# Long scans and an earlier gate row in the mLSTM gate chain, and the operand loads of the second MLP product on another queue

## The chip, the core and the metric

The kernel runs on one core of a Trainium2 chip. The core has a matrix engine (TensorE, PE in the profile), three engines for elementwise work (VectorE or DVE, ScalarE or ACT, GpSimd or POOL), and a fifth, SyncE or SP, which here only issues DMA transfers; ScalarE can issue them too. Each engine works through its instructions in order, and semaphores hold it where it needs another's result. The metric is the device time of one execution in microseconds, the median of several runs.

## The reference, cut to what matters

```python
def _layer(x, c_act, ...):                      # x: 1024 positions x 1024, one sequence
    sh1, sc1, g1, sh2, sc2, g2 = split(c_act @ w_ada + b_ada, 6)
    h = ln(x) * (1 + sc1) + sh1
    q, k, v, o, fz, gates = split(h @ w_in)
    mix = concat([mlstm(q, k, v, o, gates), fourier(fz)]) @ w_out
    x = ln_affine(ALPHA * x + (1 + g1) * mix, ln1_g, ln1_b)
    h2 = ln(x) * (1 + sc2) + sh2
    ff = square(relu(h2 @ w_ff1 + b_ff1)) @ w_ff2 + b_ff2      # 1024 -> 4096 -> 1024
    return ln_affine(ALPHA * x + (1 + g2) * ff, ln2_g, ln2_b)

# in mlstm, for each of 4 heads and two directions, chunk after chunk of 128 positions:
    b = cumsum(log_f)                  # within the chunk
    g = b[-1] - b + log_i
    m_new = max(b[-1] + m, g.max())    # running stabiliser
    C = exp(b[-1] + m - m_new) * C + sum_s exp(g - m_new)[s] * k[s] v[s]^T
```

The cumulative sums of the forget gate, the running maximum of log_i - b, the per-chunk stabiliser m and the exponentials that come from them are the gate chain. All values are float32.

## The kernel before

Every float32 product is done as three matmuls on numbers split in a high and a low half: hi by hi (line 133), hi by lo (line 134), lo by hi (line 135). A split is a cast to the high half on ScalarE (line 1204 in the second MLP product) and a subtraction for the low half on VectorE (line 1205).

The stages follow one another: layer norm and modulation, its transpose, the products with w_in, the gate chain, the chunk states C and the mLSTM output per head, the Fourier groups, w_out, layer norm, the first MLP product, the second MLP product, layer norm. The order of the instructions on each engine is made by a scheduler with a timeline of its own, within the dependencies of the code; so code that is written in another place need not stand in another place on an engine, and an edit in one place can shift instructions elsewhere.

**Gate chain (lines 449 to 536).** Forget gates Fz and input gates I are transposed to 64 rows (32 forward, 32 backward) by 1024 positions, and copied out of PSUM (line 456). Lines 461 to 464 make log_sigmoid. The sums are taken chunk by chunk, 128 positions at a time: 16 scans of 32x128 (lines 468 and 470), a subtraction (line 472), and 16 more for the maximum (lines 476 and 478). Then come steps of 8 elements per row (lines 489 to 499), the maximum of cm with m0 (line 507), and the row I (line 506), which TensorE transposes (line 522). With what comes of that, VectorE makes kw (line 559) and the states C (lines 574 and 578); line 634 is the first product with the states. While the chain runs, TensorE does products with w_in that were kept for that time.

**Second MLP product (lines 1195 to 1348).** The product is computed by seven smaller products p, in the order 1, 2, 5, 6, 3, 7, 4. Each has eight units u, a unit has a left operand (hraw, read back from hid_d in DRAM, line 1221) and a right one (raw, from w_ff2, line 1212), both split, and 24 matmuls. The left loads are all issued by ScalarE, the right ones by SP. After p = 1 the code loads the layer norm's rows lg2 and lb2, makes the gate row g2 (line 680, from b_ada and g), gb = b_ff2 * g2 (line 1344), and loads the eight tiles acc with x2, each followed by acc = ALPHA * acc + gb (line 1347). gb lies in one of the three buffers of the raw loads.

Of the kernel before, what the change touches and what calls it, by code (L numbers as in the profile page):

```python
# [9 lines left out]
F32 = mybir.dt.float32  # L10
F32R = mybir.dt.float32r
AF = mybir.ActivationFunctionType
ALU = mybir.AluOpType

P = 128
D = 1024
# [74 lines left out]
def body(ctx, tc, x, c, w_ada, b_ada, w_in, b_gate, norm_w, w_out, ln1_g, ln1_b,  # L91
# [359 lines left out]
    for k_, dst in ((1, Fz), (0, I)):  # L451
        for hf in range(2):
            pt = bank("c")
            for i in range(4):
                nc.tensor.transpose(out=pt[0:64, i * P:(i + 1) * P], in_=zg[:, hf * 4 + i, k_, :], identity=ident)
            nc.vector.tensor_copy(out=dst[0:64, hf * 512:hf * 512 + 512], in_=pt[0:64, :])
# [9 lines left out]
    for n in range(NC):  # L466
        f, r_ = slice(n * P, n * P + P), slice(n * P + P - 1, n * P - 1 if n else None, -1)
        nc.vector.tensor_tensor_scan(out=br[0:32, f], data0=on[0:32], data1=Fr[0:32, f], initial=0.0,
                                     op0=ALU.mult, op1=ALU.add)
        nc.vector.tensor_tensor_scan(out=br[32:64, r_], data0=on[32:64], data1=Fr[32:64, r_], initial=0.0,  # L470
                                     op0=ALU.mult, op1=ALU.add)
    nc.vector.tensor_sub(out=a_, in0=a_, in1=br)
    cm = Fr
    for n in range(NC):
        f, r_ = slice(n * P, n * P + P), slice(n * P + P - 1, n * P - 1 if n else None, -1)
        nc.vector.tensor_tensor_scan(out=cm[0:32, f], data0=a_[0:32, f], data1=a_[0:32, f], initial=-3e38,
                                     op0=ALU.max, op1=ALU.max)
        nc.vector.tensor_tensor_scan(out=cm[32:64, r_], data0=a_[32:64, r_], data1=a_[32:64, r_], initial=-3e38,
                                     op0=ALU.max, op1=ALU.max)
# [26 lines left out]
    nc.vector.tensor_tensor(out=I[64:128].rearrange("p (n t) -> p n t", t=P), in0=a_v, in1=bcn(mx), op=ALU.subtract)  # L506
    nc.vector.tensor_tensor(out=cmv, in0=cmv, in1=bcn(m0), op=ALU.max)
# [709 lines left out]
    def left(p, u):  # L1217
        nraw[0] += 1
        pl, t_, n_ = ((r2, "hraw", 2), (opp, "op4", 2))[nraw[0] // 2 % 2] if nraw[0] > 2 else (xp, "raw", 3)
        raw = pl.tile([P, 2, 512], F32, name="hraw", tag=t_, bufs=n_)  # L1220
        nc.scalar.dma_start(out=raw, in_=hid_d[p - 1, 2 * u:2 * u + 2].rearrange("n p d -> p n d"))
        return raw
# [90 lines left out]
    for n_, p in enumerate((1, 2, 5, 6, 3, 7, 4)):  # L1313
        pbs = [bank(t_) for t_ in ("aabc", "abbc")[n_ % 2]]
        late = NLAST if p == 4 else 0
        for u in range(NU - late):
# [3 lines left out]
            if p == 3:  # L1320
                raw = w2_raw(u, 1, 0)
                nc.vector.tensor_sub(out=tt[u], in0=raw, in1=tt[u])
            if p == 7 and u % 2:
                for ch in range(2):
                    ln2_part(u // 2, ch)
                ln2(u // 2)
# [10 lines left out]
        if n_ == 0:  # L1337
            lg2, lb2 = [r2.tile([P, D], F32, name=n) for n in ("lg2", "lb2")]
            nc.sync.dma_start(out=lg2, in_=bc1(ln2_g))
            nc.sync.dma_start(out=lb2, in_=bc1(ln2_b))  # L1340
            gate_rows(1, g2)
            gb = xp.tile([P, D], F32, name="gb", tag="raw", bufs=3)
            nc.sync.dma_start(out=gb, in_=bc1(b_ff2))
            nc.vector.tensor_mul(out=gb, in0=gb, in1=g2)
            for st in range(NST):
                nc.sync.dma_start(out=acc[st], in_=x2_d[st * P:st * P + P, :])
                nc.vector.scalar_tensor_tensor(out=acc[st], in0=acc[st], scalar=ALPHA, in1=gb, op0=ALU.mult,  # L1347
                                               op1=ALU.add)
# [25 lines left out]
```

## Time and profile before

| | |
|---|---|
| median of 3 runs | 1109.8 us (1107.94 to 1109.94) |
| the profiled execution, its own time | 1109.07 us |
| its span, first to last instruction | 1107.3 us |
| TensorE busy | 1042.8 us (94%) |
| VectorE busy | 775.9 us (70%) |
| ScalarE busy | 469.4 us (42%) |
| GpSimd busy | 319.6 us (29%) |
| mean granted TensorE clock | 0.965 of 2.4 GHz |

TensorE is the engine that is nearly always busy, so the time goes where it idles or where its clock is at the lower of its two levels (0.50 of full speed, 1.2 GHz). The shares of the other engines are means over stages that differ; whether VectorE matters is seen only in the stretch where TensorE waits for it. All start times below are microseconds from the start of the span.

### The profile page before, as it was taken

Reading aid. Unit: us, or ns where it says so; the run is one execution under the profiler, and the core shown is the slowest. Engines: PE = TensorE matmul, PEld = TensorE weight load, DVE = VectorE, ACT = ScalarE, POOL = GpSimd, SP = SyncE. Lnnn points to the kernel's source line nnn. Section 1 sums busy time; section 2 is a strip of 40 time slices with the busy share of each in tenths; the row PEclk is TensorE's granted clock in tenths of the full one; section 3 lists DMA queues with packets and bytes.
Section 4 is the critical chain, followed back from the end, with each engine's and each line's share of the span. In section 5 each row is a group of like instructions: output and inputs, shape, how many; then the busy total and the mean of one; then the engine's idle time right before and its main releaser. Section 6 shows DMA issues by size and latency. Waiting matters only on the chain.

```text
span 1107.3 us, 14282 instructions
## 1 busy us (share of the span) xinstructions
PE 1042.8 (94%) x5033; PEld 857.1 (77%) x5033; DVE 775.9 (70%) x1431; ACT 469.4 (42%) x812; POOL 319.6 (29%) x247
## 2 busy tenths in 40 slices
PE   5899989999899898879999999999989999999995
PEld 3788978898677687668888888888868888888884
DVE  7943785967779488878565445445476896668997
ACT  3353125654355115676455445354344333333420
POOL 3554205532124011002777766752200000000000
PEclk7999989989899899989999999999999999999998
DMA  9926604432224802854566564546978885688402
GB/s 307 290 60 216 195 28 122 132 115 89 82 65 137 284 39 102 251 180 125 162 212 206 180 206 150 178 152 204 340 282 288 266 308 190 218 271 282 163 30 93
DMA packets 146887, 199.31 MB, mean 180 GB/s; under 512 B 9392, under 2 KB 74876, under 8 KB 146816
## 3 DMA queue, kind: packets, MB, share of 16 engines
q1 hardware_dynamic: 126688, 162.22, 44.7%
q10 hardware_dynamic: 20128, 36.18, 9.7%
q8 instruction: 39, 0.64, 0.2%
q14 instruction: 32, 0.26, 0.1%
HBM read 153.01 MB, written 45.36 MB: 179 GB/s over the span
## 4 chain that ended last, share of the span: by engine, by line
PE 57%; DVE 2%; ACT 1%; DMA 0%; issue 0%; DVEq 0%; ACTq 0%
PE psb L134 7%; PE psb L135 7%; PE psb L133 7%; PE psa L133 7%; PE psa L134 7%; PE psa L135 7%; PE psc L134 5%; PE psc L135 5%; PE psc L133 5%; DVE acc L1347 0%; PE psc L933 0%; DMA rw<-in_w_ff_dram 0%; DVE acc L1304 0%; ACT b L937 0%; ACT w L955 0%
## 5 line engine op out<-in xcount | busy, mean ns | idle before, releaser
L1204 ACT CAST o<-hraw 128x1024 fp32r<-128x1024 f32 x56 | 58.6, 1050 | 137.1 <-PE psc L135 107.5
L1205 DVE TENSOR_TENSOR o<-hraw,o 128x1024 fp32r<-128x1024 f32 x56 | 70.5, 1265 | 42.2 <-ACT o L1204 42.2
L133 PE MATMUL psa<-wh,hR 128*128 128x256 f32 (+2 forms) x268 | 81.0, 303 | 0.6 <-DVE acc L892 0.6
L135 PE MATMUL psa<-wh,hR 128*128 128x256 f32 (+2 forms) x268 | 79.9, 298 | 0.0
L134 PE MATMUL psa<-wl,hR 128*128 128x256 f32 (+2 forms) x268 | 79.4, 297 | 0.0
L134 PE MATMUL psa<-o,o 128*128 128x512 f32 x176 | 69.3, 394 | 5.9 <-DVE o L1205 5.9
L135 PE MATMUL psa<-o,o 128*128 128x512 f32 x176 | 69.4, 394 | 0.0
L133 PE MATMUL psa<-o,o 128*128 128x512 f32 x176 | 68.9, 393 | 0.0
L978 ACT ACTIVATE hq<-hq 128x512 f32<-128x512 f32 x59 | 37.1, 629 | 62.2 <-DVE hq L974 61.4
L134 PE MATMUL psb<-o,o 128*128 128x512 f32 x160 | 62.9, 393 | 0.0
L135 PE MATMUL psb<-o,o 128*128 128x512 f32 x160 | 62.8, 393 | 0.0
L133 PE MATMUL psb<-o,o 128*128 128x512 f32 x160 | 62.4, 392 | 0.0
L263 POOL TENSOR_TENSOR wl<-raw,wh 128x256 fp32r<-128x256 f32 (+2 forms) x27 | 38.0, 1430 | 73.8 <-ACT wh L262 73.8
L133 PEld LDWEIGHTS psa<-wh,hR 128*128 128x128 f32 x268 | 52.6, 196 | 2.7 <-DVE acc L892 1.3
L134 PEld LDWEIGHTS psa<-wl,hR 128*128 128x128 f32 x268 | 52.6, 196 | 2.0 <-issue 0.9
L135 PEld LDWEIGHTS psa<-wh,hR 128*128 128x128 f32 x268 | 52.4, 196 | 1.0
L1047 DVE TENSOR_TENSOR ws<-raw,ws 128x1024 fp32r<-128x1024 f32 x30 | 39.6, 1333 | 13.8 <-ACT ws L1046 13.8
L418 POOL TENSOR_TENSOR m<-m,mraw 128x512 f32<-128x512 f32 x28 | 39.5, 1412 | 29.6 <-ACT m L415 10.3
L1037 POOL TENSOR_TENSOR raw<-raw 128x512 f32<-128x512 f32 x15 | 21.3, 1418 | 90.4 <-DVE w L1112 86.2
L1204 ACT CAST o<-raw 128x1024 fp32r<-128x1024 f32 x32 | 33.3, 1048 | 31.4 <-DVE raw L1247 18.2
L1171 POOL TENSOR_TENSOR hq<-hq 128x512 f32<-128x512 f32 x16 | 22.7, 1418 | 78.1 <-ACT hq L979 62.1
L134 PEld LDWEIGHTS psa<-o,o 128*128 128x128 f32 x176 | 33.3, 189 | 13.7 <-DVE o L1205 6.3
(437 smaller groups left out, 3150.6 us busy)
## 6 DMA issues: line engine op xcount, KB each, us to landing
raw<-in_w_ff_dram SPq DMA_DIRECT2D x104, 512.0 KB, 4.8
hraw<-hid_d ACTq DMA_DIRECT2D x56, 512.0 KB, 4.8
hid_d<-hq SPq DMA_DIRECT2D x107, 256.0 KB, 3.2
mraw<-in_w_ada_dram SPq DMA_DIRECT2D x32, 512.0 KB, 4.2
raw<-in_w_in_dram SPq DMA_DIRECT2D x10, 512.0 KB, 3.9
xt<-in_x_dram SPq DMA_DIRECT2D x8, 512.0 KB, 5.3
wa<-in_w_ada_dram SPq DMA_DIRECT2D x16, 256.0 KB, 5.2
wa<-in_w_ada_dram SPq DMA_DIRECT2D x8, 512.0 KB, 8.1
```

The source lines that it names most:

```text
L133: nc.tensor.matmul(out=out_ap, lhsT=lh, rhs=rh, start=first, stop=False)
L134: nc.tensor.matmul(out=out_ap, lhsT=lh, rhs=rl, start=False, stop=False)
L135: return nc.tensor.matmul(out=out_ap, lhsT=ll, rhs=rh, start=False, stop=last)
L263: nc.gpsimd.tensor_sub(out=wl, in0=raw, in1=wh)
L418: nc.gpsimd.tensor_add(out=mc, in0=mc, in1=rv[:, i])
L978: nc.scalar.activation(out=h_, in_=h_, func=AF.Relu)
L1037: eng.tensor_add(out=r1[:, hi], in0=r1[:, lo], in1=r1[:, hi])
L1047: nc.vector.tensor_sub(out=w_[:, 1], in0=s_, in1=w_[:, 0])
L1171: nc.gpsimd.tensor_add(out=sa, in0=h12, in1=h22)
L1204: nc.scalar.copy(out=o_[:, 0], in_=raw)
L1205: eng.tensor_sub(out=o_[:, 1], in0=raw, in1=o_[:, 0])
```

## The change

In the gate chain the two copies of I out of PSUM go to ScalarE; the 32 scans over a chunk each become four over all 1024 positions, in which a mask tile, keep, restarts the sum or the maximum at the start of each chunk; and the row I comes ahead of the maximum over cm. In the second MLP product all left loads but the first three are issued by SP; gb has a place of its own, which lb2 takes over later; the eight loads of acc and their additions are written into the loops of p = 2 and p = 5; lg2 and lb2 are loaded after p = 6.

```diff
@@ gate chain
-            nc.vector.tensor_copy(out=dst[0:64, hf * 512:hf * 512 + 512], in_=pt[0:64, :])
+            (nc.vector.tensor_copy if k_ else nc.scalar.copy)(out=dst[0:64, hf * 512:hf * 512 + 512], in_=pt[0:64, :])
...
-    for n in range(NC):
-        f, r_ = slice(n * P, n * P + P), slice(n * P + P - 1, n * P - 1 if n else None, -1)
-        nc.vector.tensor_tensor_scan(out=br[0:32, f], data0=on[0:32], data1=Fr[0:32, f], initial=0.0,
-                                     op0=ALU.mult, op1=ALU.add)
-        nc.vector.tensor_tensor_scan(out=br[32:64, r_], data0=on[32:64], data1=Fr[32:64, r_], initial=0.0,
-                                     op0=ALU.mult, op1=ALU.add)
+    keep = md.tile([64, 2, S], F32, name="keep")
+    for w_, (rest, start) in enumerate(((1.0, 0.0), (0.0, -3e38))):
+        nc.gpsimd.memset(keep[:, w_], rest)
+        nc.gpsimd.memset(keep[:, w_].rearrange("p (n t) -> p n t", t=P)[:, :, 0:1], start)
+
+    def scans(out, src, which, initial, op0, op1):
+        for rs, r_ in ((slice(0, 32), slice(None)), (slice(32, 64), slice(None, None, -1))):
+            nc.vector.tensor_tensor_scan(out=out[rs, r_], data0=keep[rs, which], data1=src[rs, r_], initial=initial,
+                                         op0=op0, op1=op1)
+
+    scans(br, Fr, 0, 0.0, ALU.mult, ALU.add)
     nc.vector.tensor_sub(out=a_, in0=a_, in1=br)
     cm = Fr
...
+    scans(cm, a_, 1, -3e38, ALU.add, ALU.max)
...
-    nc.vector.tensor_tensor(out=I[64:128].rearrange("p (n t) -> p n t", t=P), in0=a_v, in1=bcn(mx), op=ALU.subtract)
-    nc.vector.tensor_tensor(out=cmv, in0=cmv, in1=bcn(m0), op=ALU.max)
+    i_op = nc.vector.tensor_tensor(out=I[64:128].rearrange("p (n t) -> p n t", t=P), in0=a_v, in1=bcn(mx),
+                                   op=ALU.subtract)
+    with tc.issue_after(i_op.ins):
+        nc.vector.tensor_tensor(out=cmv, in0=cmv, in1=bcn(m0), op=ALU.max)
@@ second MLP product
-        pl, t_, n_ = ((r2, "hraw", 2), (opp, "op4", 2))[nraw[0] // 2 % 2] if nraw[0] > 2 else (xp, "raw", 3)
+        pl, t_, n_ = ((opp, "op4", 2), (r2, "hraw", 2))[nraw[0] // 2 % 2 == 0] if nraw[0] > 1 else (xp, "raw", 3)
         raw = pl.tile([P, 2, 512], F32, name="hraw", tag=t_, bufs=n_)
-        nc.scalar.dma_start(out=raw, in_=hid_d[p - 1, 2 * u:2 * u + 2].rearrange("n p d -> p n d"))
+        (nc.scalar if nraw[0] <= 3 else nc.sync).dma_start(out=raw, in_=hid_d[p - 1, 2 * u:2 * u + 2].rearrange("n p d -> p n d"))
...
+            if p in (2, 5) and u % 2:
+                st = u // 2 + (4 if p == 5 else 0)
+                nc.sync.dma_start(out=acc[st], in_=x2_d[st * P:st * P + P, :])
+                nc.vector.scalar_tensor_tensor(out=acc[st], in0=acc[st], scalar=ALPHA, in1=gb, op0=ALU.mult,
+                                               op1=ALU.add)
...
-        if n_ == 0:
-            lg2, lb2 = [r2.tile([P, D], F32, name=n) for n in ("lg2", "lb2")]
+        if p == 1:
+            gate_rows(1, g2)
+            gb = r2.tile([P, D], F32, name="gb", tag="gb", bufs=1)
+            nc.sync.dma_start(out=gb, in_=bc1(b_ff2))
+            nc.vector.tensor_mul(out=gb, in0=gb, in1=g2)
+        if p == 6:
+            lg2 = r2.tile([P, D], F32, name="lg2")
+            lb2 = r2.tile([P, D], F32, name="lb2", tag="gb", bufs=1)
             nc.sync.dma_start(out=lg2, in_=bc1(ln2_g))
             nc.sync.dma_start(out=lb2, in_=bc1(ln2_b))
-            gate_rows(1, g2)
-            gb = xp.tile([P, D], F32, name="gb", tag="raw", bufs=3)
-            nc.sync.dma_start(out=gb, in_=bc1(b_ff2))
-            nc.vector.tensor_mul(out=gb, in0=gb, in1=g2)
-            for st in range(NST):
-                nc.sync.dma_start(out=acc[st], in_=x2_d[st * P:st * P + P, :])
-                nc.vector.scalar_tensor_tensor(out=acc[st], in0=acc[st], scalar=ALPHA, in1=gb, op0=ALU.mult,
-                                               op1=ALU.add)
```

How the two programs stand on the engines is shown at three places. In these rows the line comes first (lines of the changed kernel run 3 to 6 higher from the gate chain on), then the operation, what it writes and what it reads, and the shape; x2 is two alike in a row, and a scan is listed as SCALAR_TENSOR_TENSOR.

VectorE before, in the gate chain, from the end of the second 16 scans to the copies that the transposes feed:

```order
L476 SCALAR_TENSOR_TENSOR Fz<-I 32x128
L478 SCALAR_TENSOR_TENSOR Fz<-I 32x128
L489 COPY G<-Fz 32x8 x2
L492 SCALAR_TENSOR_TENSOR ms<-G,bL 32x8
L494 SCALAR_TENSOR_TENSOR ms<-G,bL 32x8
L496 COPY m_1328<-ms 32x8
L497 COPY m_1328<-ms 32x8
L498 TENSOR_TENSOR mx<-m_1328,G 64x8
L507 TENSOR_TENSOR Fz<-Fz,m_1328 64x1024
L499 TENSOR_TENSOR dec<-m_1328,mx 64x8
L506 TENSOR_TENSOR I<-I,mx 64x1024
L511 TENSOR_TENSOR wi<-m_1328,Fz 64x1024
```

The same place of the changed kernel:

```order
L474 SCALAR_TENSOR_TENSOR Fz<-keep,I 32x1024 x2
L490 COPY G<-Fz 32x8 x2
L493 SCALAR_TENSOR_TENSOR ms<-G,bL 32x8
L495 SCALAR_TENSOR_TENSOR ms<-G,bL 32x8
L497 COPY m_1305<-ms 32x8
L498 COPY m_1305<-ms 32x8
L499 TENSOR_TENSOR mx<-m_1305,G 64x8
L500 TENSOR_TENSOR dec<-m_1305,mx 64x8
L507 TENSOR_TENSOR I<-I,mx 64x1024
L510 TENSOR_TENSOR Fz<-Fz,m_1305 64x1024
L514 TENSOR_TENSOR wi<-m_1305,Fz 64x1024
```

Two scans stand for sixteen, and I is written ahead of the maximum over cm (Fz). On TensorE the transposes of I (line 522, 525 in the changed kernel) come behind 163 matmuls counted from the first transpose of the gates (line 455), before 192; between them and the first matmul for kw (line 555) stand 96 matmuls, before 72.

VectorE before, at the end of p = 1; o8_7529, o8_7495 and o8_7563 are the left operands of units 1, 0 and 2 of p = 2, o8_7500 is the right one of unit 0:

```order
L1205 TENSOR_TENSOR o8_7426<-hraw_7424,o8_7426 128x1024
L1205 TENSOR_TENSOR o8_7529<-hraw_7527,o8_7529 128x1024
L1205 TENSOR_TENSOR o8_7495<-hraw_7493,o8_7495 128x1024
L1205 TENSOR_TENSOR o8_7563<-hraw_7561,o8_7563 128x1024
L680 SCALAR_TENSOR_TENSOR g2_7173<-g2_7173,raw_7467 128x1024
L1344 TENSOR_TENSOR gb_7470<-gb_7470,g2_7173 128x1024
L1347 SCALAR_TENSOR_TENSOR acc20_7149<-acc20_7149,gb_7470 128x1024
...
L1347 SCALAR_TENSOR_TENSOR acc27_7156<-acc27_7156,gb_7470 128x1024
L1205 TENSOR_TENSOR o8_7500<-raw_7498,o8_7500 128x1024
```

The same place of the changed kernel; here o8_7452, o8_7486 and o8_7522 are the left operands of units 0, 1 and 2, and o8_7457 is the right one of unit 0:

```order
L1208 TENSOR_TENSOR o8_7403<-hraw_7401,o8_7403 128x1024
L1208 TENSOR_TENSOR o8_7452<-hraw_7450,o8_7452 128x1024
L1208 TENSOR_TENSOR o8_7486<-hraw_7484,o8_7486 128x1024
L683 SCALAR_TENSOR_TENSOR g2_7150<-g2_7150,raw_7440 128x1024
L1349 TENSOR_TENSOR gb_7443<-gb_7443,g2_7150 128x1024
L1208 TENSOR_TENSOR o8_7522<-hraw_7520,o8_7522 128x1024
L1329 SCALAR_TENSOR_TENSOR acc20_7126<-acc20_7126,gb_7443 128x1024
...
L1329 SCALAR_TENSOR_TENSOR acc27_7133<-acc27_7133,gb_7443 128x1024
L1208 TENSOR_TENSOR o8_7457<-raw_7455,o8_7457 128x1024
```

The eight additions stand together in both, between a left split of unit 2 and the right split of unit 0; g2 and gb have moved ahead of the left split of unit 2.

SP's queue before, from the last but one load of acc to the second right load of p = 2:

```order
L1346 DMA acc26_7155<-x2_d_3975 128x1024
L1177 DMA hid_d_3977<-hq_7122 128x512
L1346 DMA acc27_7156<-x2_d_3975 128x1024
L679 DMA raw_7467<-in_b_ada_dram 128x1024
L1343 DMA gb_7470<-in_b_ff2_dram 128x1024
L1212 DMA raw_7498<-in_w_ff2_dram 128x2x512
L1212 DMA raw_7532<-in_w_ff2_dram 128x2x512
```

The same stretch of the changed kernel:

```order
L1328 DMA acc26_7132<-x2_d_3952 128x1024
L1180 DMA hid_d_3954<-hq_7104 128x512
L1224 DMA hraw_7450<-hid_d_3954 128x2x512
L1224 DMA hraw_7484<-hid_d_3954 128x2x512
L1180 DMA hid_d_3954<-hq_7105 128x512
L1328 DMA acc27_7133<-x2_d_3952 128x1024
L1353 DMA lg2_8346<-in_ln2_g_dram 128x1024
L1180 DMA hid_d_3954<-hq_7099 128x512
L682 DMA raw_7440<-in_b_ada_dram 128x1024
L1224 DMA hraw_7520<-hid_d_3954 128x2x512
L1215 DMA raw_7455<-in_w_ff2_dram 128x2x512
L1215 DMA raw_7489<-in_w_ff2_dram 128x2x512
```

The left loads hraw now stand in this queue between the loads of acc, b_ada and the right loads; gb's load stands ahead of all loads of acc, lb2's behind the additions. ScalarE has no load left to issue there.

## Rows read from the trace of the kernel before

**Rows 1.** The page, span and busy time: us, share of span, instructions.

```profile
span 1107.3 us, 14282 instructions
...
PE 1042.8 (94%) x5033; PEld 857.1 (77%) x5033; DVE 775.9 (70%) x1431; ACT 469.4 (42%) x812; POOL 319.6 (29%) x247
```

**Rows 2.** Waits of TensorE: line waited for: us in total, times, longest.

```profile
PE psa L134 <- DVE o L1205: 5.9, 1, 5.9
...
PE psc L522 <- DVE I L506: 5.4, 1, 5.4
...
PE psc L555 <- DVE kw L559: 1.6, 1, 1.6
```

**Rows 3.** Stretches: us, busy of PE, PEld, DVE, ACT, POOL, clock, DMA share, GB/s.

```profile
162.01:166.10 4.09, 4.09 (x19) 4.09 (x20) 2.53 (x4) 2.86 (x4) 0.47 (x1) 0.50 0.00 0
193.00:200.00 7.00, 7.00 (x62) 6.96 (x61) 6.04 (x19) 5.71 (x14) 1.54 (x2) 1.00 0.25 90
218.00:227.60 9.60, 9.59 (x46) 8.92 (x47) 5.59 (x16) 3.67 (x8) 4.02 (x4) 0.50 0.55 148
780.12:823.90 43.78, 43.78 (x194) 36.02 (x193) 24.78 (x20) 18.51 (x21) 6.45 (x4) 1.00 0.99 366
785.00:815.00 30.00, 30.00 (x133) 24.65 (x132) 13.24 (x11) 10.00 (x10) 5.89 (x4) 1.00 1.04 404
830.90:835.10 4.20, 4.20 (x10) 3.33 (x11) 4.14 (x4) 1.04 (x1) 0.00 (x0) 0.50 0.80 276
```

**Rows 4.** Timeline of TensorE, end of p = 1: start, duration, instruction, [idle before].

```profile
824.60 0.40 PE L133 MATMUL psc<-o,o 128*128 128x512 f32 x1
830.90 0.80 PE L134 MATMUL psa<-o,o 128*128 128x512 f32 x1 [5.90 <-DVE o L1205]
```

**Rows 5.** Timeline of VectorE, end of p = 1.

```profile
816.88 1.23 DVE L1205 TENSOR_TENSOR o<-hraw,o 128x1024 fp32r<-128x1024 f32 x1 [1.58 <-ACT o L1204]
818.02 1.22 DVE L680 SCALAR_TENSOR_TENSOR g<-g,raw 128x1024 f32<-128x1024 f32 x1
820.54 9.17 DVE L1347 SCALAR_TENSOR_TENSOR acc<-acc,gb 128x1024 f32<-128x1024 f32 x8
829.62 1.22 DVE L1205 TENSOR_TENSOR o<-raw,o 128x1024 fp32r<-128x1024 f32 x1
```

**Rows 6.** Timeline of VectorE, gate chain.

```profile
142.96 0.41 DVE L468 TENSOR_TENSOR_SCAN e__1287<-ones,Fz 32x128 f32<-32x128 f32 x1
...
149.37 0.41 DVE L470 TENSOR_TENSOR_SCAN e__1287<-ones,Fz 32x128 f32<-32x128 f32 x1
...
158.56 0.16 DVE L492 TENSOR_TENSOR_SCAN ms<-G,bL 32x8 f32<-32x8 f32 x1
...
159.42 1.21 DVE L507 TENSOR_TENSOR Fz<-Fz,m 64x1024 f32<-64x1024 f32 x1
...
160.74 1.22 DVE L506 TENSOR_TENSOR I<-I,mx 64x1024 f32<-64x1024 f32 x1
...
180.08 1.42 DVE L559 TENSOR_TENSOR kw<-psc,wk 128x256 f32<-128x256 f32 x4 [0.19 <-PE psc L555]
```

**Rows 7.** Timelines of ScalarE and SP (queues ACTq, SPq), end of p = 1.

```profile
814.20 1.50 ACTq L1221 DMA_DIRECT2D hraw<-hid_d  x2
...
815.79 1.05 ACT L1204 CAST o<-hraw 128x1024 fp32r<-128x1024 f32 x1 [1.94 <-DVE o L1205]
...
807.71 0.33 SPq L679 DMA_DIRECT2D raw<-in_b_ada_dram  x1
```

**Rows 8.** Timelines of VectorE, GpSimd and TensorE, the states C.

```profile
203.41 3.87 DVE L578 SCALAR_TENSOR_TENSOR C<-C,dcol 64x129 f32<-64x129 f32 x14 [0.60 <-ACT C L570]
...
209.33 5.71 DVE L578 SCALAR_TENSOR_TENSOR C<-C,dcol 64x129 f32<-64x129 f32 x4
...
210.05 4.84 POOL L263 TENSOR_TENSOR wl<-raw,wh 128x1024 fp32r<-128x1024 f32 x2
...
218.01 1.22 PE L634 MATMUL psb<-C,qw 64*128 64x129 f32 x6 [0.39 <-DVE C L578]
```

**Rows 9.** Waits of SP's queue.

```profile
SPq L1212 <- DVE o L1205: 70.1, 24, 19.9
```

More of the change, by code (lines that the diff above doesn't have):

```diff
@@ L465, in body @@
     br = e_
-    for n in range(NC):
-        f, r_ = slice(n * P, n * P + P), slice(n * P + P - 1, n * P - 1 if n else None, -1)
-        nc.vector.tensor_tensor_scan(out=br[0:32, f], data0=on[0:32], data1=Fr[0:32, f], initial=0.0,
-                                     op0=ALU.mult, op1=ALU.add)
-        nc.vector.tensor_tensor_scan(out=br[32:64, r_], data0=on[32:64], data1=Fr[32:64, r_], initial=0.0,
-                                     op0=ALU.mult, op1=ALU.add)
+    keep = md.tile([64, 2, S], F32, name="keep")
[7 more added lines that the diff above has]
+    scans(br, Fr, 0, 0.0, ALU.mult, ALU.add)
     nc.vector.tensor_sub(out=a_, in0=a_, in1=br)
     cm = Fr
[L474 to L479, printed above, removed]
+    scans(cm, a_, 1, -3e38, ALU.add, ALU.max)
     G = a2.tile([64, NC], F32, name="G")
```

## The prediction, made before the changed kernel ran

> **What bounds the kernel now.** I read the page's busy table first: TensorE works in 1042.8 of 1107.3 us [rows 1], so only what stops it, or halves its clock, can be worth much. Next the waits of TensorE, longest first. Two of the long ones lie where the change works: 5.9 us for DVE's low half o, and 5.4 us for the transposes of I; a third, 1.6 us for kw, is there to be compared [rows 2]. Then I went to these two places in the timelines and in the table of stretches, which gives the granted clock.
>
> *Second MLP product.* The first of its seven products, p = 1, ran 192 matmuls (8 units of 24) in 43.78 us at the full clock: 5.47 us a unit, no idle at all [rows 3]. At its end four matmuls hi by hi of p = 2 still ran, the last at 824.60, and then nothing until 830.90 [rows 4]. What held DVE is in its own rows: a split of a left operand at 816.88, the gate row g, gb, and then eight ALPHA additions in one piece, 820.54 to 829.71, ahead of the one split that TensorE waited for [rows 5]. After the gap the matmuls ran at clock 0.50 (the 1.2 GHz level) for 4.20 us [rows 3], half of it lost: 2.1 us. The place costs 5.9 + 2.1 = 8.0 us.
>
> *Gate chain.* DVE does 32 short scans, 16 between 142.96 and 149.8 at a pitch of 0.427 us and 16 like them after the subtraction, then the small per-chunk steps, the maximum over cm (159.42) and only then the row I (160.74) [rows 6]. TensorE waits 5.4 us for it [rows 2] and then runs 4.09 us at clock 0.50 [rows 3]: 2.05 us lost, 7.4 us at this place.
>
> **Part one, the gate chain.** Scans: one of 8 elements takes 0.16, one of 128 takes 0.41 [rows 6], so (0.41 - 0.16)/120 = 2.08 ns an element, and 1024 elements come to 0.16 + 1016 x 0.00208 = 2.28 us. The other bound is eight of the short ones, 3.28. The row nearest in kind is the slope, since both points are scans of 32 rows; I take 2.3. Four are 9.1 against 32 x 0.427 = 13.7: 4.5 us off (bound 0.5). I ahead of the maximum: 160.74 - 159.42 less the 0.15 step that stays ahead of it, 1.2 us. So I is done near 161.96 - 5.7 = 156.3. The two copies of I to ScalarE cost nothing: on DVE they stood under the exponential and the logarithm, and on ScalarE one goes ahead of that pair and one behind it; if that cover were gone it would be a ScalarE copy of 64x512, at most the 1.27 us that DVE's two share. The four memsets of the mask are on GpSimd near 92 to 96 us, where it has nothing to do.
>
> What TensorE gets of the 5.7 is less. In the new order the transposes stand 29 matmuls earlier; at 7.00/62 = 0.113 us each [rows 3] TensorE arrives 3.3 us sooner, at 153.3, and waits 3.0 us. That is longer than the wait of 1.6 us [rows 2], behind which the clock stayed at 1.00 [rows 3], and shorter than 5.4, behind which it fell; I assume that it falls again. Then 24 of the 29 matmuls come between the transposes and the first kw, so kw starts near 177 instead of 180.08 [rows 6], or 175 if the clock holds: 3 to 5 us sooner. From there DVE is what is late: it works almost without a gap until the first product with the states C, at 218.01 [rows 8], and it has the same steps to do: 37.9 us. That matmul thus comes at 213 to 215, but by the new order TensorE has by then 30 or so matmuls, 3.4 us, less behind it. Net: 3 to 5 less 3.4, from -0.4 to 1.6. Behind 218.01 the clock is 0.50 for 9.60 us [rows 3], 4.8 us lost, and nothing in the change removes the gap ahead of it. I take **1 us** for the part; its bounds are -4 (one more such fall of the clock) and +6 (no fall at 162 or at 218).
>
> **Part two, the loads of the second MLP product.** In the code the eight additions now stand spread over two products; the order shows them still in one piece, ahead of the split of p2u0's right operand. So what counts is when the piece starts. Before, g and gb (1.22 each) came behind the last of three left splits, p2u2, at 816.88 [rows 5]. That split was late because ScalarE's queue held two hraw loads, 1.50 us at 814.20, that waited for a buffer of DVE's; the cast stood behind them until 815.79 [rows 7]. After, the loads are on SP's queue, and g and gb stand ahead of p2u2. Four steps:
> 1. b_ada, which g needs, was issued at 807.71 [rows 7]. With gb moved earlier, lb2 moved behind and the hraw loads in the same row, some 11 MB stand up to it from 780.5 on; at 404 GB/s, the DMA engines full [rows 3], that is 28 us: it lands near 810. g and gb: done by 813.
> 2. p2u2's cast needs the operand buffer of p1's unit 5, free two units before 824.1, at 813.1. Cast 1.05 [rows 7] and split 1.23 [rows 5] (they overlap by 0.1): 815.3.
> 3. Eight additions, 9.17 [rows 5]: 824.5. Split of p2u0: 825.7.
> 4. TensorE wants it at 824.60 + 0.23 = 824.8: a wait of 0.9 us, below the 1.6 that left the clock alone.
> So 5.9 - 0.9 + 2.1 = **7.1 us**. Bounds: if p2u2's split stays at 816.88, the piece runs 818.1 to 827.3, the split ends at 828.5, TensorE waits 3.7 and the clock falls: 2.2 us. If there is no wait at all: 8.0. I take 7.1, since each step's wait has its row and the two causes, g and gb behind and the loads in ScalarE's queue, are both gone from the order.
>
> A rule speaks against the second of these. The row first: ScalarE spent 1.50 us on two issues, and its cast waited 1.94 [rows 7]. The Trainium skill, "DMA: Bandwidth & Descriptors", section "Issuing engines are not separate DMA queues", says that issuing from several engines saves only the sequencer's issue time, since all transfers share the same 16 engines. Taken alone it would give p2u2 back 1.5 us at most and the time of the first rival; the row shows an issue that also waits for a buffer, which the rule does not count.
>
> The loads of hraw now wait in SP's queue with all the others; what stands behind them there is the raw loads. lg2 and lb2 are used last of all and cost nothing where they go. The raw slot that gb held is free, which can only help. For the later products the list of TensorE's waits names none, and nothing there changes but the queue.
>
> **Rivals.**
> *The piece stays late (1).* A buffer or a landing still holds p2u2's split at 816.9, or b_ada lands after 815. Against: the rows above; for: the piece is not spread, and the DMA engines are full until 815. Then B is 2.2 to 4 us: 1109.8 - 2.2 - 1 = 1106.6, down to 1104.
> *The gate chain pays in full (2).* The clock holds behind the shorter wait (2.05) or behind 218 (4.8), so the part brings 5 to 7: 1109.8 - 7.1 - 6 = 1096.7. For: the waits get shorter. Against: DVE's steps with C take 0.28 us alone (14 in 3.87) but 1.43 (4 in 5.71) while GpSimd works on wl [rows 8]; these follow GpSimd's timing, not the chain's.
> *Nothing in sum (3).* The change does not do what it says: the piece stays late, and the 29 matmuls moved behind the transposes are missing as cover later, with one more fall of the clock (-2 to -4): 1108 to 1112.
> *Slower (4).* SP's queue is in order. Raw loads waited in it 70.1 us in 24 waits for DVE's splits, the longest 19.9 [rows 9]; hraw loads on their own queue did not. Now one such wait holds hraw loads. The left splits stand three units ahead, 16.4 us. A wait of 19.9 would run 3.5 us over, and a fall of the clock like the 2.1 above makes 5.6. One is covered by the gain; from two on the kernel is slower: 1109.8 - 8.1 + 11.2 = 1112.9. Against: in the new SP order the loads stand in the order in which DVE frees the buffers.
>
> **How the numbers follow.** Sum: 7.1 + 1 = 8.1 us off. Against the profiled run of 1109.07 (span 1107.3 and 1.8 outside it) that is 1101.0; the median of the runs is 0.7 above that run, so I forecast 1101.7. Chances: the forecast (1099 to 1104) 0.50; rival 1 (1104 to 1107.5) 0.18; rival 2 (1094.5 to 1099) 0.12; rival 3 0.10; rival 4 (above 1112) 0.10. The range takes the first three: 1094.5 to 1107.5. About 0.2%, 2.2 us, is what a measurement can tell here; faster 0.50 + 0.18 + 0.12 = 0.80, same 0.10, slower 0.10.
>
> **What would show it.** Right: TensorE's wait for DVE's o at the start of p = 2 is under 1.6 us and the clock there stays 1.00; scans of about 2.3 us; a wait of about 3 us at the transposes with clock 0.50 behind it; the first product with C at 213 to 215. Wrong: eight additions that start after 817; scans near 3.3; TensorE waiting for o or for hraw anywhere later in the seven products; a clock of 1.00 behind the transposes or behind the products with C, or a new stretch of 0.50 between 160 and 300.

## The result, and the profile after

The changed kernel takes 1097.12 us (median of 4 runs, 1096.39 to 1098.13) against 1109.5 us for the kernel before, now the median of 4 runs: a ratio of 0.9892, interval 0.9874 to 0.9909, 12.4 us by the medians. The forecast was 1101.7 us, with a range of 1094.5 to 1107.5: the sign and the range held, the size was 8 where 12 came, outside the 1099 to 1104 us that stood for the forecast itself, and the two parts of the sum were both off, in opposite directions.

The page of after, span and busy time:

```profile
span 1095.4 us, 14286 instructions
...
PE 1038.6 (95%) x5033; PEld 853.8 (78%) x5033; DVE 766.8 (70%) x1401; ACT 470.2 (43%) x814; POOL 324.6 (30%) x251
```

The span is 11.9 us shorter than in [rows 1], and TensorE is only 4.2 us less busy: the rest is idle time. The waits of TensorE in after (line waited for: us in total, times, longest):

```profile
PE psc L525 <- DVE I L507: 3.4, 1, 3.4
...
PE psc L609 <- DVE qw L601: 2.5, 1, 2.5
PE psa L134 <- DVE o L1208: 2.0, 1, 2.0
```

Against [rows 2]: 5.4 became 3.4 at the transposes of I, 5.9 became 2.0 at the second product, and the 1.6 for kw is gone from the list. Stretches of after (length, busy of PE, PEld, DVE, ACT, POOL, clock, DMA share, GB/s):

```profile
156.17:161.90 5.73, 5.73 (x27) 5.73 (x28) 3.75 (x5) 1.53 (x4) 0.00 (x0) 0.50 0.00 0
161.90:170.00 8.10, 8.10 (x61) 6.64 (x59) 0.19 (x1) 2.39 (x4) 5.69 (x6) 1.00 0.20 55
214.60:224.00 9.40, 9.33 (x68) 8.47 (x69) 6.88 (x24) 5.78 (x14) 5.68 (x5) 1.00 0.48 142
772.52:816.30 43.78, 43.78 (x194) 36.02 (x192) 30.17 (x24) 19.77 (x22) 7.44 (x4) 1.00 0.97 366
820.60:824.10 3.50, 3.50 (x10) 2.71 (x10) 3.28 (x3) 0.00 (x0) 0.00 (x0) 0.51 0.84 265
```

The clock still falls behind the transposes (first row; 2.9 us lost, 2.05 before), does not fall behind the 2.5 us wait at 214.6 (third row, where 4.8 us were lost in [rows 3]), and falls again at the second product (last row, 1.7 us lost, 2.1 before). The fourth row is p = 1, as long as before to the hundredth; it starts at 772.52 where it started at 780.12. So 7.6 us of the gain were made before the second product (0.4 of them before the gate chain began), and 11.9 - 7.6 = 4.3 us in it. The forecast had 1 and 7.1. The 7.6 is the difference of two single executions and carries their chance: in the seven traces that have TensorE's order of after (named with the second trace of before, below), p = 1 starts 4.5 to 9.0 us ahead of the first trace of before, and in the second trace of before 2.3 us behind it. The medians of the gate part alone, below, are the better figure for part one: 5.8 us.

VectorE in the gate chain of after (start, duration, instruction, [idle before]):

```profile
142.61 4.59 DVE L474 TENSOR_TENSOR_SCAN e__1287<-keep,Fz 32x1024 f32<-32x1024 f32 x2
...
148.74 4.59 DVE L474 TENSOR_TENSOR_SCAN Fz<-keep,I 32x1024 f32<-32x1024 f32 x2
...
154.90 1.22 DVE L507 TENSOR_TENSOR I<-I,mx 64x1024 f32<-64x1024 f32 x1
156.15 1.22 DVE L510 TENSOR_TENSOR Fz<-Fz,m 64x1024 f32<-64x1024 f32 x1
...
177.85 0.76 DVE L562 TENSOR_TENSOR kw<-psc,wk 128x256 f32<-128x256 f32 x2 [0.57 <-PE psc L558]
```

These answer to [rows 6]: two scans take 4.59 us, 2.3 each, I is done at 156.12, and kw starts at 177.85. TensorE's rows that belong to it, the last answering to [rows 8]:

```profile
156.17 1.97 PE L525 MATMUL psc<-cs,I 128*128 128x128 f32 x8 [3.37 <-DVE I L507]
...
207.58 0.94 PE L637 MATMUL psb<-C,qw 64*128 64x129 f32 x10
...
214.67 0.47 PE L609 MATMUL psc<-RM,cr 128*128 128x512 f32 x1 [2.51 <-DVE qw L601]
```

The first product with C comes at 207.58, where it came at 218.01. The last row is the wait of 2.5 us for qw. Before, it came ahead of the first product with C and of the stretch at clock 0.50 behind that product, and it was shorter:

```profile
216.61 0.47 PE L606 MATMUL psc<-RM,cr 128*128 128x512 f32 x1 [2.13 <-DVE qw L598]
```

VectorE at the end of p = 1 in after:

```profile
805.38 1.22 DVE L683 SCALAR_TENSOR_TENSOR g<-g,raw 128x1024 f32<-128x1024 f32 x1 [2.72 <-DMA raw<-in_b_ada_dram]
806.64 1.22 DVE L1349 TENSOR_TENSOR gb<-gb,g 128x1024 f32<-128x1024 f32 x1
807.90 1.23 DVE L1208 TENSOR_TENSOR o<-hraw,o 128x1024 fp32r<-128x1024 f32 x1
809.04 9.17 DVE L1329 SCALAR_TENSOR_TENSOR acc<-acc,gb 128x1024 f32<-128x1024 f32 x8
818.12 2.35 DVE L1208 TENSOR_TENSOR o<-raw,o 128x1024 fp32r<-128x1024 f32 x2
```

In what follows p2u0 is unit 0 of p = 2, and so on; the split in the third row is that of p2u2's left operand. These rows answer to [rows 5], and the first is new: VectorE waits 2.72 us for b_ada. From the order of [rows 5], moved up by the 7.6 us that the kernel is ahead, the additions start 820.54 - 7.6 - 809.04 = 3.9 us earlier, and the wait of TensorE is 5.90 - 2.00 = 3.9 us shorter.

### The profile page after: what moved, and what is told of

Its sections match the earlier page's. It is cut to its first block, busy times and chain, and to the rows that moved or that the text cites. A ratio compares the mean times of both kernels' runs of the same rounds, so it can differ in the third digit from the quotient of the medians.

```text
span 1095.4 us, 14286 instructions
## 1 busy us (share of the span) xinstructions
PE 1038.6 (95%) x5033; PEld 853.8 (78%) x5033; DVE 766.8 (70%) x1401; ACT 470.2 (43%) x814; POOL 324.6 (30%) x251
## 4 chain that ended last, share of the span: by engine, by line
PE 53%; DMA 3%; DVE 2%; ACT 2%; issue 1%; POOL 1%; ACTq 0%; DVEq 0%; POOLq 0%
PE psb L134 7%; PE psb L135 7%; PE psb L133 7%; PE psa L135 6%; PE psa L133 6%; PE psa L134 6%; PE psc L134 5%; PE psc L135 5%; PE psc L133 5%; DMA raw<-in_w_ff_dram 1%; DMA hid_d<-eh 1%; DMA s_d<-es 1%; DMA rw<-in_w_ff_dram 0%; ACT b L940 0%; PE psc L936 0%
## 5 line engine op out<-in xcount | busy, mean ns | idle before, releaser
L133 PE MATMUL psa<-wh,hR 128*128 128x256 f32 (+2 forms) x268 | 79.1, 296 | 1.0 <-DVE acc L895 1.0
L135 PE MATMUL psa<-wh,hR 128*128 128x256 f32 (+2 forms) x268 | 77.9, 291 | 0.0
L133 PEld LDWEIGHTS psa<-wh,hR 128*128 128x128 f32 x268 | 51.3, 191 | 3.9 <-DVE acc L895 1.5
L135 PEld LDWEIGHTS psa<-wh,hR 128*128 128x128 f32 x268 | 51.4, 192 | 0.8
L418 POOL TENSOR_TENSOR m<-m,mraw 128x512 f32<-128x512 f32 x28 | 36.5, 1307 | 34.2 <-ACT m L415 19.2
L1208 DVE TENSOR_TENSOR o<-raw,o 128x1024 fp32r<-128x1024 f32 x32 | 39.9, 1256 | 8.0 <-ACT o L1207 7.8
```

Source lines behind the costliest of these rows:

```text
L133: nc.tensor.matmul(out=out_ap, lhsT=lh, rhs=rh, start=first, stop=False)
L135: return nc.tensor.matmul(out=out_ap, lhsT=ll, rhs=rh, start=False, stop=last)
L418: nc.gpsimd.tensor_add(out=mc, in0=mc, in1=rv[:, i])
L1208: eng.tensor_sub(out=o_[:, 1], in0=raw, in1=o_[:, 0])
```

## The experiments

The kernels ran in three groups, each beside the kernel before on one chip; ratios are against that. For each trace I also added up, over stretches of 2 us, TensorE's idle time (length less busy) and the time lost to the clock (busy times one less the granted clock). The table has both for the two places of the change, 130 to 300 us and 770 to 860 us; each row is one profiled execution.

| kernel | ratio (interval) | 130-300: idle, clock | 770-860: idle, clock |
|---|---|---|---|
| before | 1 | 13.1, 10.1 | 5.9, 2.1 |
| before, second trace | | 13.5, 7.7 | 5.6, 2.6 |
| second product alone | 0.9963 (0.9949 to 0.9977) | 14.3, 8.1 | 2.0, 1.7 |
| scans alone | 0.9923 (0.9906 to 0.9939) | 8.8, 7.4 | 5.7, 2.7 |
| gate part alone | 0.9944 (0.9929 to 0.9958) | 10.2, 6.2 | 6.0, 2.8 |
| after | 0.9892 (0.9874 to 0.9909) | 9.1, 6.0 | 2.0, 1.7 |
| after, second trace | 0.9885 (0.9867 to 0.9903) | 8.7, 6.3 | 1.9, 0.0 |
| after, products first | 0.9880 (0.9859 to 0.9902) | 9.8, 5.0 | 2.1, 0.0 |
| after, g2 early | 0.9868 (0.9853 to 0.9884) | 8.7, 6.0 | 0.0, 0.0 |
| after, left loads on ScalarE | 0.9873 (0.9856 to 0.9891) | 8.7, 6.2 | 1.0, 0.0 |
| after, additions spread | 0.9876 (0.9858 to 0.9895) | 10.0, 6.3 | 0.0, 0.0 |
| after, g2 early, loads on ScalarE | 0.9913 (0.9896 to 0.9930) | 9.1, 6.2 | 1.9, 0.0 |
| after, products first, g2 early | 0.9857 (0.9840 to 0.9874) | 8.8, 7.4 | 0.0, 0.0 |

**Gate part alone.** The kernel before with the hunks of lines 453 to 510 of the diff.

> The kernel before with the gate-chain part alone. Theory: the two parts add up, and the trace of after puts 7.5 us on this part: the shorter wait at the transposes of I (5.4 to 3.4 us), the wait for kw gone (1.6), and no stretch at clock 0.50 behind the first product with C (4.8). It should read 1102, with clock 1.00 from 207 to 225. Rival: the missing fall of the clock was chance, or came with the other part: then the clock falls again behind 214, and the time is 1105 to 1107.

Measured 1102.77 us against 1108.56: 5.8 us. The theory's time, and the clock neither as the theory nor as the rival had it: behind the wait at 214 it fell, but for a short time only (1.7 us lost between 200 and 240, against 5.0 in the first trace of before). At the second product this trace shows the 6.0 us wait of before.

**Second product alone.** The kernel before with the other hunks.

> The kernel before with the part on the second MLP product alone. Theory: the parts add, and this one gives the 4.3 us by which the lead grew over the second product in the trace of after: 1105.2, a wait of TensorE for the right split of about 2 us, then a clock near 0.50 for 3.5 us. Rival: the prediction's working, 7.1 us, was right for this part and something else took 2.8 of it in after: 1102.4, a wait under 1 us with the clock at 1.00.

Measured 1105.14 us, 3.4 us by the medians and 4.1 by the ratio: the theory. The wait is 1.95 us and the clock falls behind it (1.7 us). VectorE shows the same wait for b_ada:

```profile
814.00 1.23 DVE L680 SCALAR_TENSOR_TENSOR g<-g,raw 128x1024 f32<-128x1024 f32 x1 [2.71 <-DMA raw<-in_b_ada_dram]
815.26 1.23 DVE L1346 TENSOR_TENSOR gb<-gb,g 128x1024 f32<-128x1024 f32 x1
816.52 1.22 DVE L1205 TENSOR_TENSOR o<-hraw,o 128x1024 fp32r<-128x1024 f32 x1
```

The product of the two ratios is 0.9907, within the interval of the whole (0.9874 to 0.9909) and near its end: the parts add, as far as can be measured.

**g2 early.** After, with the gate row and gb ahead of the loop over p.

```diff
+    gate_rows(1, g2)
+    gb = r2.tile([P, D], F32, name="gb", tag="gb", bufs=1)
+    nc.sync.dma_start(out=gb, in_=bc1(b_ff2))
+    nc.vector.tensor_mul(out=gb, in0=gb, in1=g2)
     for n_, p in enumerate((1, 2, 5, 6, 3, 7, 4)):
...
-        if p == 1:
-            gate_rows(1, g2)
...
```

> After, with the gate row g2 and gb (their three loads and two steps) written ahead of the seven products instead of behind p = 1. Theory: in after the eight additions start late because b_ada lands late in full DMA queues (VectorE waited 2.7 us for it), so with b_ada loaded early the additions are done before p = 2, TensorE does not wait there, the clock stays at 1.00: 2.0 + 1.7 = 3.7 us less than after, 1093.4. Rival: what holds TensorE is the 9.2 us of additions on VectorE wherever they stand, or the loads shift and something else is late: 1096 to 1099, with a wait of TensorE on another split in p = 1 or p = 2.

Measured 1094.52 us, 0.9868. In its trace the additions stand one or two at a time between the splits of p = 1 (three of the seven rows):

```profile
785.76 1.21 DVE L1333 SCALAR_TENSOR_TENSOR acc<-acc,gb 128x1024 f32<-128x1024 f32 x1
...
798.06 1.23 DVE L1333 SCALAR_TENSOR_TENSOR acc<-acc,gb 128x1024 f32<-128x1024 f32 x1 [0.88 <-DMA acc<-x_d]
802.80 1.22 DVE L1333 SCALAR_TENSOR_TENSOR acc<-acc,gb 128x1024 f32<-128x1024 f32 x1
```

TensorE has no idle time at all between 770 and 860 and no fall of the clock. That the wait came from the late piece of additions is shown. That b_ada alone made the piece late is not: the edit spread the additions as well. The gain over after is 0.2% by the ratios, with intervals that overlap.

**Left loads on ScalarE.** After, with one line back.

```diff
-        (nc.scalar if nraw[0] <= 3 else nc.sync).dma_start(out=raw, ...)
+        nc.scalar.dma_start(out=raw, ...)
```

> After, with all left loads issued by ScalarE again as before. Theory of the prediction: loads that wait in ScalarE's queue hold its casts, so splits come later and TensorE waits more at p = 2: 1099 to 1101. Rival: the queue that issues them does not matter, and in this order the right split of unit 0 stands ahead of the eight additions and that of unit 1 behind them: the wait at unit 0 goes, or moves one unit on, 1093 to 1097.

Measured 1094.88 us, 0.9873: the rival. What [rows 7] showed is there again, two issues of 1.50 us and a cast that comes 1.94 us late (first two rows). The additions start 3.2 us later than in after, though this execution reached p = 1 1.4 us sooner, since g, gb and the right split of unit 0 now all stand behind the split that this cast feeds. But with that right split ahead of the additions, the delay costs little:

```profile
804.88 1.50 ACTq L1224 DMA_DIRECT2D hraw<-hid_d  x2
...
806.48 1.05 ACT L1207 CAST o<-hraw 128x1024 fp32r<-128x1024 f32 x1 [1.94 <-DVE o L1208]
...
811.10 1.22 DVE L1208 TENSOR_TENSOR o<-raw,o 128x1024 fp32r<-128x1024 f32 x1
812.24 9.17 DVE L1329 SCALAR_TENSOR_TENSOR acc<-acc,gb 128x1024 f32<-128x1024 f32 x8
821.33 1.21 DVE L1208 TENSOR_TENSOR o<-raw,o 128x1024 fp32r<-128x1024 f32 x1
```

So the wait stands at unit 1, whose split comes last, and is 1.04 us.

**The kernel before, a second trace.** No edit.

> The kernel before, unchanged, for a second trace. Question: is the long stretch at clock 0.50 behind the first product with C (218 to 227.6 us in the first trace, 4.8 us lost) a property of this order of work? Theory that the change removed it: it is there again, 3 to 5 us lost between 200 and 240. Rival, chance: it is short or missing, under 1 us lost, as in the traces of after and of the two kernels made from it.

One run, 1111.48 us. Between 200 and 240 it lost 2.8 us to the clock, the first trace 5.0. So the long stretch of the first trace was in part chance. Over all traces, those in the order of before (two of before, the second product alone) lose 10.1, 7.7 and 8.1 us between 130 and 300, those in the order of after (seven rows of the table, from the gate part alone on, without the two with products first) 6.0 to 6.3. By the means, 8.6 and 6.2, some 2.4 us are the change's, and between 1.4 and 4.1 by the single traces. How far two executions can differ here is seen in the two kernels with products first, which share their gate chain: 5.0 and 7.4 us.

**Products first.** After, with the loop over the last group of w_in written ahead of the transposes, and these issued behind its last matmul. TensorE then has 192 matmuls between the transposes of the gates and those of I, as before.

```diff
+    wh, wl = load_group(512)
+    for st in range(NST):
+        pb = proj_N(wh, wl, 256, st)
+        ...
     for hf in range(2):
         pt = bank("c")
         for i in range(4):
-            nc.tensor.transpose(out=pt[:, i * P:(i + 1) * P], in_=I[:, n * P:(n + 1) * P], identity=ident)
+            with tc.issue_after(last_p[0].ins):
+                nc.tensor.transpose(out=pt[:, i * P:(i + 1) * P], in_=I[:, n * P:(n + 1) * P], identity=ident)
```

> After, with the products of the last group of w_in written ahead of the transposes of I and the transposes issued behind them, so that TensorE's order there is that of the kernel before: 192 matmuls ahead of the transposes, not 163. Theory: TensorE then arrives when I is done, so the wait of 3.4 us and the clock fall behind it (2.9 us lost) go, and idle time does not come back later since VectorE starts on kw no later: 6 us less than after, 1091. Rival, the step of the prediction: the matmuls moved ahead are missing as cover while VectorE works on kw and C, so TensorE waits 3 us more between 175 and 215, and the time is 1095 to 1098.

Measured 1097.57 us, 0.9880, as after (0.9885 and 0.9892): the rival. The wait at the transposes is gone and the clock stays at 1.00 behind them, and others have come. The waits of TensorE from 125 to 300 us in this kernel:

```profile
PE psb L641 <- ACT tb L668: 2.4, 1, 2.4
PE psc L562 <- DVE kw L566: 2.1, 1, 2.1
PE psc L613 <- DVE qw L605: 2.1, 1, 2.1
PE psb L641 <- DVE C L585: 1.5, 1, 1.5
PE psc L540 <- ACT wk L537: 0.8, 1, 0.8
PE psb L573 <- DVE kw L566: 0.5, 1, 0.5
...
```

And from 125 to 300 us in after:

```profile
PE psc L525 <- DVE I L507: 3.4, 1, 3.4
PE psb L637 <- ACT tb L664: 2.6, 1, 2.6
PE psc L609 <- DVE qw L601: 2.5, 1, 2.5
...
```

Idle and clock together are 14.8 us between 130 and 300 here and 15.1 in after. In this kernel, where the 29 matmuls stand decides where TensorE waits for VectorE, hardly how long.

**Scans alone.** The kernel before with the mask and the four scans, I behind the maximum and its copies on VectorE as before.

> The kernel before with the four long scans alone: copies of I on VectorE and the maximum ahead of I as before, the second product as before. Theory: the scans give their 4.5 us of the chain's 5.7, and the time follows the chain: 0.8 of the 5.8 us that the gate part gave alone, 1104. Rival: the step that counts is I ahead of the maximum, the rest is absorbed: 1107 or above.

Measured 1102.51 us against 1110.48: 8.0 us, no less than the whole gate part. VectorE and TensorE in this kernel:

```profile
155.62 1.21 DVE L507 TENSOR_TENSOR Fz<-Fz,m 64x1024 f32<-64x1024 f32 x1
156.93 1.22 DVE L506 TENSOR_TENSOR I<-I,mx 64x1024 f32<-64x1024 f32 x1
...
158.21 1.97 PE L522 MATMUL psc<-cs,I 128*128 128x128 f32 x8 [3.31 <-DVE I L506]
```

I comes 2.0 us later than in after, 1.0 of it because this execution was 1.0 us behind when the gates were transposed; the other 1.0 goes with the maximum, which stands ahead of I. TensorE waits 3.31 us against 3.37: the scheduler had put 172 products ahead of the transposes, nine more than in after. The copies of I on VectorE cost the chain nothing: the scans start 11.0 us after the first transpose of the gates in this kernel as in after (10.9 before). A difference from the gate part in favour of the scans alone (0.9923 against 0.9944) is not shown, the intervals overlap; that I ahead of the maximum brings anything is not shown either.

**Products first and g2 early.**

> After, with both edits: products ahead of the transposes, and g2 and gb ahead of the seven products. Theory: the two places are independent, so the gains against after add, 6 us and the 2.6 us that the second gave alone: 1088.5. Rival: they share a cause (or the first gives nothing): 1092 to 1095.

Measured 1094.80 us, 0.9857: the rival, as g2 early alone (0.9868). The products' place again brings nothing that can be measured.

**After again, and two kernels beside it.** The changed kernel on the chip of the next two.

> The changed kernel, unchanged, beside the next two on one chip. It should read 0.989 of before (0.9874 to 0.9909 measured first), with the wait of TensorE for the right split at p = 2 near 2.0 us again.

Measured 1095.15 us, 0.9885, the wait 1.93 us. This time the clock stayed at 1.00 behind it.

**Additions spread.** After, with each addition tied behind the right split of its unit (line 1328).

```diff
-                nc.vector.scalar_tensor_tensor(out=acc[st], in0=acc[st], scalar=ALPHA, in1=gb, op0=ALU.mult,
-                                               op1=ALU.add)
+                with tc.issue_after(last_s[0].ins):
+                    nc.vector.scalar_tensor_tensor(out=acc[st], in0=acc[st], scalar=ALPHA, in1=gb, op0=ALU.mult,
+                                                   op1=ALU.add)
```

> After, with each of the eight additions to acc tied behind the right split of its own unit, so that they stand spread over p = 2 and p = 5 on VectorE, one for every second unit, and the left loads stay on SP's queue. Theory: the piece of eight additions is all that TensorE still waits for at p = 2: wait 0, clock 1.00 there, 3.7 us less than after, 0.9855 of before. Rival: the left loads on SP's queue, behind the right ones, are what is late (in the kernel with the loads back on ScalarE the wait was 1.0 us without a fall of the clock): a wait of 1 to 2 us stays or moves to a later unit, 0.988 to 0.989.

Measured 1094.70 us, 0.9876. The wait is gone and none took its place in the seven products, with b_ada as late as in after and the left loads on SP's queue: what TensorE still waited for in after was the piece. The first of the spread additions, and VectorE's wait for b_ada, in this kernel:

```profile
808.50 1.23 DVE L683 SCALAR_TENSOR_TENSOR g<-g,raw 128x1024 f32<-128x1024 f32 x1 [2.68 <-DMA raw<-in_b_ada_dram]
...
812.30 1.23 DVE L1208 TENSOR_TENSOR o<-raw,o 128x1024 fp32r<-128x1024 f32 x1
...
818.27 1.22 DVE L1330 SCALAR_TENSOR_TENSOR acc<-acc,gb 128x1024 f32<-128x1024 f32 x1
```

The gain over after on the same chip, 0.1% by the ratios, is below what was expected and below what these runs can tell: in the trace of after beside it the place had cost 1.9 us, without a fall of the clock, and the end of this kernel has 0.7 us more idle time.

**g2 early and left loads on ScalarE.** Both edits above.

> After, with g2 and gb ahead of the seven products and all left loads issued by ScalarE. Each alone took the clock fall and at least half of the wait at p = 2 away. Theory: they are two ways round the same 3.7 us, so together they give no more than one: 0.986 of before. Rival: the left loads on ScalarE's queue hold its casts, as the prediction said, now that no other order hides it: TensorE waits for splits in p = 1 or p = 2, 0.989 or above.

Measured 1098.79 us, 0.9913 (0.9896 to 0.9930): the rival, against 0.9868 and 0.9873 of the single edits. TensorE and ScalarE's rows in p = 1:

```profile
797.54 0.49 PE L133 MATMUL psa<-o,o 128*128 128x512 f32 x1 [0.91 <-ACT o L1207]
798.99 0.50 PE L134 MATMUL psa<-o,o 128*128 128x512 f32 x1 [0.95 <-DVE o L1208]
...
793.19 2.25 ACTq L1224 DMA_DIRECT2D hraw<-hid_d  x2
795.49 1.05 ACT L1207 CAST o<-hraw 128x1024 fp32r<-128x1024 f32 x1 [9.13 <-DMA acc<-x_d]
```

ScalarE computes nothing for 9.13 us, at the end of which it issues two left loads (2.25 us), and only then casts; TensorE waits for that cast and for the split behind it. With the loads on SP's queue (g2 early alone) these waits are not there. They explain 1.9 of the 4 to 5 us by which the ratios differ. The two profiled executions are 5.1 us apart: 2.4 us of that came within p = 1, and 2.7 us before it, nearly all between 410 and 520 us, where no edit stands. So a good part is the chance of single executions; whether all of the rest of the ratio is, is open, and it is not tested that the issues alone held the cast.

## Why the prediction was right or wrong

**The sign, and that the start of the piece decides: right.** The additions still stood in one piece, g and gb ahead of p2u2's split, and the wait shrank by what the piece came earlier, 3.9 us both. Of the two causes that the prediction named, the place of g and gb is borne out: with the two behind that split again (left loads on ScalarE) the additions start 3.2 us later. The loads in ScalarE's queue held the cast, but for less than forecast, and with the late cast back the time (0.9873) was no worse than after's.

**Its size, 7.1 us: wrong at steps 1 and 2, both times in when a load lands.** Step 1 had b_ada there near 810, which is 802.4 in after's time, 7.6 us ahead. Step 2 had p2u2's cast wait for an operand buffer until 813.1, 805.5 in after's time. In after the cast waits for something else, its own left load, which SP now issues right behind b_ada:

```profile
797.02 0.33 SPq L682 DMA_DIRECT2D raw<-in_b_ada_dram  x1
797.64 0.37 SPq L1224 DMA_DIRECT2D hraw<-hid_d  x1
...
806.81 1.05 ACT L1207 CAST o<-hraw 128x1024 fp32r<-128x1024 f32 x1 [5.41 <-DMA hraw<-hid_d]
```

VectorE could go on with b_ada at 805.38, 8.4 us after its issue, and ScalarE with the left load at 806.81, 9.2 us after its own, with a DMA share of 0.97 over p = 1. gb and the cast both end at 807.86, so either of the two loads alone would have held the split of p2u2 at 807.90. That split was to end at 815.3 (807.7 in after's time), and the additions were to start there; they started at 809.04, 1.3 us late by the forecast. The wait was 2.0 and not 0.9, and the clock fell behind it in two of the four traces with a wait near 2 us there (after and the second product alone; not in after's second trace nor with products first). 3.9 + 0.4 = 4.3 instead of 5.0 + 2.1. That is little above what rival 1 had for this place, 2.2 to 4 us when a landing holds p2u2's split. The forecast's lower bound, 2.2, and its upper, 8.0, held the value.

**The gate chain: the steps right, the sum wrong.** The scans (2.3 forecast, 2.30 measured), I at 156.3 (156.12), the wait at the transposes (3.0; 3.37), the fall of the clock behind it, and kw at 177 (177.85) all came as worked out. What failed are the next two steps. The first is that from kw to the first product with C VectorE "has the same steps to do: 37.9 us". It took 29.7 us, since fewer steps stand ahead of that product in the new order: two with qw and not four, and on the second line with C 16 and not 22, the two that run beside GpSimd's steps of wl now being behind the product (before, then after; the number behind the bar is their time in us):

```profile
L578 DVE SCALAR_TENSOR_TENSOR C<-C,dcol 64x129 f32<-64x129 f32 x22 | 13.0, 680 | 0.7 <-ACT C L570 0.6
L581 DVE SCALAR_TENSOR_TENSOR C<-C,dcol 64x129 f32<-64x129 f32 x16 | 4.4, 399 | 0.0
```

So the product came at 207.58, not at 213 to 215. The second is "TensorE has by then 30 or so matmuls, 3.4 us, less behind it", taken off the lead there as a loss. It had 25 fewer behind it (1159 instructions of TensorE, before 1184), but only because the product had itself moved in TensorE's order. At the wait for qw, where VectorE holds TensorE in both kernels, the lead is 1.9 us (214.67 against 216.61), and the changed kernel has 12 instructions more behind it there (1192, before 1180), not 30 fewer. The 29 matmuls put behind the transposes were not missing later; they stood where TensorE had waited for kw (1.6 us in [rows 2], and 0.5 us further down the same list). The kernel with the products first shows it from the other side: with the order of before these waits are back, 2.1, 0.5 and 1.5 us, and the time is the same. The fair measure was idle time: 13.1 to 9.1 us between 130 and 300, 4 us, and some 2.4 us of clock, about 6 in all, as the gate part alone gave (5.8), at the upper end of the part's range (-4 to 6).

The time is that of the second rival, which had 0.12, but its mechanism came only in part, and partly by chance. It took the gain of 5 to 7 us from the clock, and by these means more than half came as idle time. Behind the transposes the clock did not hold. Behind 214 it held in four of the seven traces with TensorE's order of after and fell for a shorter time in three (1.7 us lost), although the wait ahead of it was longer than before, 2.5 and not 2.1 us; why it fell less is not shown. The rival's "Against" also rests on a mean that mixes two things: of the four steps with C of 1.43 us in [rows 8], two took 2.5 us, each beside one step of wl, and two 0.6 and 0.4 us; and the steps of 0.28 us were not all alone, GpSimd worked on m from 205.00 on.

**The rule weighed against the change.** The Trainium skill, "DMA: Bandwidth & Descriptors", section "Issuing engines are not separate DMA queues", counts as the gain of a second issuing engine only the time on the sequencer that it takes to initiate a DMA. The prediction took from it that p2u2 gets back 1.5 us at most, and in after that came true: counted from the start of p = 1 its cast came at 35.7 us before, at 34.3 in after and at 35.4 with the left loads back on ScalarE. So the other queue was worth 1.1 to 1.4 us to the cast, where step 2 had 2.7, and the order that came with the loads on ScalarE made up for that. With g2 early it was otherwise: moving the loads to ScalarE took the ratio from 0.9868 to 0.9913, with TensorE waiting 1.9 us in p = 1, first for the cast at the end of the 9.13 us above and then for the split behind it; the two issues themselves took 2.25.

**The slower rival** did not show: from p = 2's first unit on, the list of waits of after names no wait of TensorE for a split or a left load.

## What to carry to other kernels

When a scheduler reorders, do not take a moved instruction as the milestone of a lead: compare idle time, and time at the lower clock, stage by stage. Here the shortened chain on the engine that TensorE waits for came through, the time being the same whether the freed matmuls stood ahead of the wait or behind it. Code written "when due" may need an edge to hold it there: here the scheduler put eight additions back into one piece, and either loading their inputs early or tying each to a split took away the last wait; these versions read 0.1 to 0.3% better than the change, the best (products first and g2 early) 0.9857 of before, none clear of it. And ask of every step in a sum which load it waits for, and what is issued ahead of that load: two steps here were late by a load.

## What the runs showed of the hardware

Whether the clock falls behind a wait of about 2 us differed between executions of one program: in after it was 0.51 for 3.5 us behind a wait of 2.00 us in one trace and 1.00 behind 1.93 us in the other, and a wait of 2.5 us at 214.6 was followed by 1.00. In the first 130 us, where the edits add no more than four memsets on GpSimd, the time lost to the clock was 1.6 us in the trace of the gate part alone and 7.3 us in that of the last kernel above. By these two a single trace does not price the clock's falls in such a stretch to better than some 3 us, half of their difference.

A load of 512 KB took 8.4 us (b_ada) and 9.2 us (p2u2's left operand) from its issue to the step that it let go on, at a DMA share of 0.97; the same row b_ada, loaded earlier in the same trace at 329.71, landed after 3.8 us.

A scan of 32 rows by 1024 took 2.30 us, and one of 32 by 128 0.41 us: the slope between short scans carried to a length eight times greater.
